# A router chain in a new order of statements, and a new end that keeps the last sums in PSUM

## The chip, the cores and the metric

The kernel runs on one core of a Trainium2 chip. The metric is the device time of one execution in microseconds (us); of three runs the median counts. A profiled execution has a span, from its first to its last recorded instruction, and a time of its own that is a little longer.

## What is computed

Two transformer blocks on 256 tokens of width 1024, in float32. The change touches the end of the second block: its mixture of 32 experts, of which a router picks four for each token, and the last normalisation.

```python
def moe_ffn(h, w_router, b_router, w1, b1, w2, b2):
    ...
    logits = (hf @ w_router + b_router).astype(jnp.float32)
    top_v, top_e = lax.top_k(logits, TOP_K)
    gates = jax.nn.softmax(top_v, axis=-1)
    ...
    def expert_block(args):
        xi, e = args
        hc = xi @ w1[e] + b1[e]
        g, u = hc[:, :D_EXPERT], hc[:, D_EXPERT:]
        g = jnp.minimum(g, SWIGLU_LIMIT)
        u = jnp.clip(u, -SWIGLU_LIMIT, SWIGLU_LIMIT)
        hm = (u + 1.0) * (g * jax.nn.sigmoid(SWIGLU_ALPHA * g))
        return hm @ w2[e] + b2[e]
...
        x = x + g1 * (mixed @ w_out[l])

        h2 = rms_norm_2(x, norm2_g[l]) * (1.0 + sc2) + sh2
        x = x + g2 * moe_ffn(h2, w_router[l], b_router[l], w_exp_in[l], b_exp_in[l], w_exp_out[l], b_exp_out[l])
    return rms_norm_2(x, final_g)
```

## The kernel before

The kernel goes through both blocks stage by stage; each stage's weights come through SyncE's DMA queue in the order of use, into a ring of seven slots of 2 MB and, for halves of the second expert weights, slots of 1 MB. A load is issued (L1116) when the instruction that last read its slot has ended. Engines run their own instructions in program order; TensorE (PE) does all products, VectorE (DVE) and ScalarE (ACT) read PSUM and do the elementwise work, GpSimd (POOL) does the powers that give reciprocal roots.

**Setup of the router.** The router's weights `wr` are multiplied once by the modulation's scale, and its constant row `crow` comes from the shift and the bias (`router_setup`, L1217). It runs as background work between other statements of block 2.

**Router.** The last product of the attention half leaves X in four PSUM banks, tile tt of 128 tokens by half of the width. `router_bank` (L1462) takes each bank as it ends: add it to X, transpose four blocks of 128 into PSUM, copy them to `xT` (which lies in `sg`), square X for the mean, and multiply with `wr` into 32 logits a token, one product for each of the eight blocks of the width. `choose` (L1451) scales the logits, finds the largest eight, their indices, and marks the four chosen in `sel`. `positions` (L1775) counts, by products with a triangle and with ones, which slot of its expert a token has; `one_hots` (L1532) makes the 64 slots' one-hot columns P, and `dispatch` (L1542) gathers the tokens for a pair of experts by products of X and P into `px`, which ACT copies with the modulation to `xe`. A row `g2` is spread over the partitions by two 512-column products between the router's logits and the positions (L167, `pc` and `ph`, with ACT copies into `rowg`).

**Experts.** The loop at L1840 goes through p = 0 to 31, two experts to a pair. Stage 1 is 16 products, `pg` and `pu` in turn for the eight blocks kt, each as two half-width tiles of the array side by side, and a bias. Stage 2 (L1640) transposes the gated rows (`ph`), copies them to `hT` and multiplies them with the second weights into `py`, whose rows 0 to 63 hold the left 512 columns and rows 64 to 127 the right ones. `scaled2` (L1683) weights `py` with `rowg` into `ys`, the even expert in rows 0 to 63, the odd one in rows 64 to 127. `combine` (L1710) adds a pair into Y by four 512-column products with the transposed gate table `pt` (`weights_T` of `Pg`), each followed by an addition on DVE. It runs a pair late, in the next even expert; for the last pair it runs at the end.

**End.** `final` (L1910) follows each of those last four additions: Y times the gain `fg`, a square with its sum, and after the fourth the mean, the power and the scale. A loop for tokens that found no slot (L1930) runs as often as a value says, and then two DMAs write the output, one from SyncE's queue and one from ACT's (L1955).

In the order's rows and the profile one helper, L167, records every float32 product; names tell them apart. A 512-column product of 128 rows shows as two records in the timeline.

## Time and profile before

| | us |
|---|---|
| median of three runs | 2325.98 (2325.09 to 2327.9) |
| profiled execution, its own time | 2323.74 |
| its span | 2321.7 |
| PE busy in the span | 2216.9 |
| DVE busy | 1261.6 |
| ACT busy | 857.4 |
| share of 16 DMA engines, SyncE's queue | 70.5% |
| router, last product of block 2's attention half to first expert product | 1364.8 to 1380.0 |
| experts 0 to 31 | 1380.0 to 2307.2 |
| end, last product to the end of the span | 2307.2 to 2321.7 |

In a timeline a row has a start, a duration, the engine, the line, the operation, what it writes and reads with its shape, how many records were put together, and in brackets how long the engine was idle ahead of it and what it waited for. PE stands for products, PEld for loading their stationary operand. A stretch's row gives busy times and, as PEclk, the granted clock as a share of 2.4 GHz.

### The profile page before, as it was taken

How to read it: one execution, taken by the hardware profiler on the slowest of the kernel's cores; microseconds unless marked ns; L12 is line 12 of the kernel's file. 1: busy time of each engine (PE TensorE's matmuls, PEld its weight loads, DVE VectorE, ACT ScalarE, POOL GpSimd, SP SyncE). 2: the span in 40 equal slices, each digit the busy share in tenths (PEclk: the TensorE clock that was granted, in tenths of full speed). 3: DMA queues.
4: the chain of work that ended last, by engine and by line, in shares of the span. 5: the costliest groups of instructions: out<-in, count | busy, mean ns of one | idle time of the engine just before them, and what ended most of it. 6: DMA issues, size and time to landing. Idle time of an engine off the chain costs nothing.

```text
span 2321.7 us, 33945 instructions
## 1 busy us (share of the span) xinstructions
PE 2216.9 (95%) x13354; PEld 1571.5 (68%) x13354; DVE 1261.6 (54%) x2338; ACT 857.4 (37%) x1535; POOL 286.4 (12%) x316
## 2 busy tenths in 40 slices
PE   8999999999999999999999999999988888999997
PEld 7889999999999988888788863333333333433332
DVE  6677668897777677876687553422222222222223
ACT  5567454545777654544554531011000000000001
POOL 3003000202777400000032010000000000000000
PEclk9999999999999999999999999999999999999999
DMA  6434555555333578886455469999999999999996
GB/s 219 160 109 146 179 186 180 182 182 182 129 130 141 199 279 285 289 285 232 166 189 200 146 235 424 407 429 429 428 429 429 428 429 429 428 419 414 429 429 260
DMA packets 71376, 654.31 MB, mean 282 GB/s; under 512 B 8176, under 2 KB 8304, under 8 KB 15920
## 3 DMA queue, kind: packets, MB, share of 16 engines
q1 hardware_dynamic: 69264, 644.91, 70.5%
q0 software_dynamic: 1664, 6.56, 0.8%
q8 instruction: 106, 1.74, 0.3%
q10 hardware_dynamic: 288, 0.67, 0.1%
q14 instruction: 54, 0.44, 0.0%
HBM read 649.61 MB, written 2.49 MB: 281 GB/s over the span
## 4 chain that ended last, share of the span: by engine, by line
PE 57%; DMA 10%; DVE 4%; ACT 3%; issue 1%; POOL 0%; ACTq 0%; POOLq 0%; DVEq 0%; SPq 0%
PE acc L153 15%; PE lin L153 11%; DMA w<-in_w_exp_in 10%; PE py L167 8%; PE pg L167 7%; PE pu L167 7%; PE psR L167 2%; PE pc L167 2%; PE px L167 2%; PE psS L167 1%; DVE lo L122 1%; ACT hT L1647 1%; DVE cv L1262 1%; ACT xe L1553 1%; DVE Pg L1561 0%
## 5 line engine op out<-in xcount | busy, mean ns | idle before, releaser
L122 DVE TENSOR_TENSOR lo<-raw,hi 128x1024 fp32r<-128x1024 f32 x411 | 519.3, 1264 | 205.2 <-PE acc L153 92.0
L119 ACT ACTIVATE hi<-raw 128x1024 fp32r<-128x1024 f32 x411 | 434.4, 1059 | 300.8 <-PE acc L153 171.9
L153 PE MATMUL lin<-hbH,hi 128*128 128x256 f32 x1152 | 329.5, 286 | 0.0
L153 PE MATMUL lin<-hbL,hi 128*128 128x256 f32 x1152 | 325.5, 283 | 0.1
L153 PE MATMUL lin<-hbH,lo 128*128 128x256 f32 x1152 | 325.4, 282 | 0.0
L1601 ACT ACTIVATE sgm<-g 128x512 f32<-128x512 f32 (+1 forms) x34 | 20.8, 612 | 726.9 <-DVE g L1600 726.9
L167 PE MATMUL pg<-w,xe 128*64 128x512 f32 x1024 | 265.0, 596 | 22.1 <-DMA w<-in_w_exp_in 22.1
L167 PE MATMUL pu<-w,xe 128*64 128x512 f32 x1024 | 263.2, 592 | 0.0
L1600 DVE TENSOR_SCALAR g<-pg 128x512 f32<-128x512 f32 (+1 forms) x33 | 22.3, 675 | 403.9 <-PE pg L167 403.9
L153 PEld LDWEIGHTS lin<-hbH,hi 128*128 128x128 f32 x1152 | 218.9, 190 | 0.2 <-ACT hbH L764 0.2
L153 PEld LDWEIGHTS lin<-hbL,hi 128*128 128x128 f32 x1152 | 216.0, 188 | 0.3 <-DVE hbL L765 0.3
L153 PEld LDWEIGHTS lin<-hbH,lo 128*128 128x128 f32 x1152 | 216.2, 188 | 0.0
L153 PE MATMUL acc<-hi,wh 128*128 128x512 f32 x512 | 200.8, 392 | 0.0
L153 PE MATMUL acc<-hi,wl 128*128 128x512 f32 x512 | 199.5, 390 | 0.7 <-DVE wl L964 0.7
L153 PE MATMUL acc<-lo,wh 128*128 128x512 f32 x512 | 199.2, 389 | 0.0
L167 PEld LDWEIGHTS pg<-w,xe 128*64 128x64 f32 x1024 | 70.4, 137 | 173.3 <-issue 127.8
L1687 DVE TENSOR_TENSOR ys<-py,rowg 64x512 f32<-64x512 f32 x62 | 42.7, 688 | 242.1 <-PE py L167 241.6
L167 PEld LDWEIGHTS pu<-w,xe 128*64 128x64 f32 x1024 | 73.7, 137 | 146.0 <-issue 138.6
L153 PE MATMUL lin<-hH,hi 128*128 128x256 f32 x552 | 167.9, 304 | 0.0
L153 PE MATMUL lin<-hH,lo 128*128 128x256 f32 x552 | 159.8, 290 | 4.0 <-DVE lo L122 4.0
L153 PE MATMUL lin<-hL,hi 128*128 128x256 f32 x552 | 159.3, 289 | 1.0 <-DVE hL L1178 1.0
L167 PE MATMUL py<-w,hT 128*64 128x512 f32 x496 | 115.6, 609 | 21.6 <-ACT hT L1647 21.6
(549 smaller groups left out, 3614.4 us busy)
## 6 DMA issues: line engine op xcount, KB each, us to landing
w<-in_w_exp_in SPq DMA_DIRECT2D x128, 2048.0 KB, 25.8
raw<-in_peer_uT SPq DMA_DIRECT2D x64, 1024.0 KB, 4.8
raw<-in_peer_v SPq DMA_DIRECT2D x64, 1024.0 KB, 6.2
raw<-in_w_exp_out SPq DMA_DIRECT2D x64, 1024.0 KB, 22.6
w<-in_w_exp_out SPq DMA_DIRECT2D x32, 2048.0 KB, 29.3
raw<-in_w_in SPq DMA_DIRECT2D x48, 1024.0 KB, 4.8
whole<-in_w_ada SPq DMA_DIRECT2D x48, 512.0 KB, 6.4
raw<-in_w_out SPq DMA_DIRECT2D x8, 1024.0 KB, 4.9
```

Of the source, the lines that this page charges most:

```text
L119: nc.scalar.activation(it["hi"], r, AF.Copy)
L122: nc.vector.tensor_tensor(out=it["lo"], in0=r, in1=it["hi"].bitcast(F32), op=OP.subtract)
L153: PE.matmul(ps, l, r, start=start and n == 0, stop=stop and n == len(trios) - 1, skip_group_check=True)
L167: PE.matmul(ps, lhsT, rhs, start=start, stop=stop, skip_group_check=True)
L1262: V.scalar_tensor_tensor(dst, x_, cw[:, b, k:k + 1], dst, op0=OP.mult, op1=OP.add)
L1553: ACT.activation(xe[:, kt].rearrange("p e c -> p (e c)"), px[:, k], AF.Identity, scale=mc[:, 2, kt:kt + 1], bias=mc[:, 3, kt:kt + 1])
L1600: V.tensor_scalar(c(g), c(pg), 7.0, None, op0=OP.min)
L1601: ACT.activation(c(sgm), c(g), AF.Sigmoid, scale=1.702)
L1647: ACT.activation(hT[:, b], ph[:, b], AF.Copy)
L1687: V.tensor_tensor(out=ys[par * C:(par + 1) * C, c], in0=py[r], in1=rowg[r, c], op=OP.mult)
```

## The change

- `router_setup` moves to block 1's PEER stage, behind the modulation's columns (L1047); it is otherwise the same.
- The router is written as one sequence of statements by hand. The transposed X lies in `aH` and `aL`. The logits come by `product`: four products at a time with a quarter of the array's columns each (32 experts by 128 tokens), then a copy and one product with four stacked identity blocks (`ones4`) that adds the quarters and transposes. `choose` marks the four by replacing the four largest values and comparing; indices are found later. One square moves from ACT to DVE. The one-hots of the first pair are made in the router, and half of the first `px` and the row g2 move into stage 1 of expert 0.
- The last expert leaves the loop. Both transposed tables, the pair's `pt` and one for the last expert alone (`pt2`, the same 64 columns in both halves of its rows), are made ahead of its stage 1. In that stage the four sums of the output are begun in four PSUM banks: Y by a product with the identity, and expert 30's rows by one with `pt`. Behind its last product one DVE operation weights all of `py` in its own layout, and four half-height products add it to the sums. Squares, gains and scales read the sums, and four ACT copies then write them to Y for the loop of extra tokens.
- Both output DMAs go through SyncE's queue.

```diff
+        def router_setup():
+
+            e = XA[:, 0].rearrange("p (k e) -> p k e", k=8)
+            er = XA[:, 1, :32]
+            GP.tensor_tensor(out=e, in0=wr, in1=mc[:, 3, :, None].to_broadcast([128, 8, 32]), op=OP.mult)
+            yield 3
+            GP.tensor_tensor(out=wr, in0=wr, in1=mc[:, 2, :, None].to_broadcast([128, 8, 32]), op=OP.mult)
+            V.tensor_reduce(out=er, in_=e.rearrange("p k e -> p e k"), axis=AX.X, op=OP.add)
+            yield 3
+            pr = psM.tile([128, 512], F32, name="psM")
+            mm(pr[:, :32], ones, er, True, False)
+            yield 1
+            mm(pr[:, :32], col("b_router_2")[:32].to_broadcast([32, 128]), ident[:32, :32], False, True)
+            yield 1
+            ACT.activation(crow, pr[:, :32], AF.Copy)
...
+        xT = [keep.tile([128, 4, S], F32, name=n) for n in ("aH", "aL")]
+        tb = [psT.tile([128, 512], F32, name="psT"), psO.tile([128, 512], F32, name="psO")]
...
+        def product(i):
+
+            tt, half = divmod(i, 2)
+            if half == 0:
+                pl[tt] = lin.tile([128, 512], F32, name="lin")
+            for k in range(4):
+                r = slice(32 * k, 32 * k + 32)
+                mm(pl[tt][r, :128], wr[:, 4 * half + k], xT[half][:, k, tt * 128:tt * 128 + 128], half == 0, half == 1)
...
+        def logits(tt):
+
+            lT = scratch("ry")[:, :128]
+            ACT.activation(lT, pl[tt][:, :128], AF.Copy)
+            mm(pl[tt][:, 128:128 + NR], lT, ones4, True, True)
...
+            V.tensor_copy(out=v4[:, tt, :4], in_=v8[:, tt, :4])
+            V.match_replace(out=eq[:, tt, 0], in_to_replace=v4[:, tt], in_values=lg[:, tt], imm_value=-3.0e38)
+            V.tensor_scalar(sel[:, tt], eq[:, tt, 0], -2.0e38, None, op0=OP.is_lt)
...
+        ended = [bank0, bank1, bank2, lambda: iter(())]
+        wide_tokens(ps, (mH, mL), 8, lambda i: bg.add(ended[i]()))
         bg.drain()
+        mean(0)
+        moved(3)
+        turn(1)
+        copy(1)
+        square(2)
+        square(3)
+        product(0)
+        turn(2)
+        product(1)
+        copy(2)
+        turn(3)
+        logits(0)
+        copy(3)
+        mean(1)
+        choose(0)
+        product(2)
+        product(3)
+        logits(1)
+        choose(1)
+        positions(0)
+        positions(1)
...
-                if kt == 0:
-                    dispatch(pair, 0, 2)
+                if kt < 2:
+                    dispatch(pair, 0, 2, kt)
...
+                    for _ in row([(psc, "pc"), (psc, "pc")], "g2", rowg):
+                        pass
...
+    p = NE - 1
+    hs = lambda dh: slice(dh * 512, dh * 512 + 512)
+    pt = weights_T(Pg)
+    cl = columns(p // 2, posm, perm[:, 0:2]), columns(p // 2, gate, perm[:, 2:4])
+
+    pt2 = weights_T(weights(*[lambda tt, e, f=f: f(tt, 1) for f in cl]))
+    last = work.tile([128, 8, 2, C], F32, name="xe").rearrange("p (a k) e c -> p a (k e c)", a=2)
+    rowg2, ysl = last[:, 0], last[:, 1]
+    for dh in range(2):
+        r = slice(64 * dh, 64 * dh + 64)
+        GP.tensor_copy(out=rowg2[r], in_=rowg[r, hs(dh)])
+    sums = [(psc if i < 2 else psx).tile([128, 512], F32, name="pc" if i < 2 else "px") for i in range(4)]
+
+    def before(kt):
+        if kt in (3, 5):
+            tt = kt // 4
+            for dh in range(2):
+                mm(sums[2 * tt + dh], ident, Y[:, tt, hs(dh)], True, False)
+                mm(sums[2 * tt + dh], pt[:C, tt], ys[:C, hs(dh)], False, False)
+
+    u = stage1(lambda kt: pair[1][:, kt, 1], ohp[:, order[p]:order[p] + 1], fetch, before, cuts=2)
+    stage2(u, fetch, None, 1, cuts=2, scaled=lambda py: V.tensor_tensor(out=ysl, in0=py, in1=rowg2, op=OP.mult))
     O = stream.rawp.tile([128, 2 * D], F32, name="raw").rearrange("p (a c) -> p a c", a=2)
     fss = wr[:, :2, :4]
+    for tt in range(2):
+        for dh in range(2):
+            r = slice(64 * dh, 64 * dh + 64)
+            mm(sums[2 * tt + dh], pt2[r, tt], ysl[r], False, True)
...
+    for f, i in ((squares, (0, 0)), (gains, (0, 0)), (squares, (0, 1)), (gains, (0, 1)), (squares, (1, 0)), (gains, (1, 0)),
+                 (squares, (1, 1)), (rstd, (0,)), (gains, (1, 1)), (scale, (0,)), (rstd, (1,)), (scale, (1,))):
+        f(*i)
+    for i in range(4):
+        ACT.activation(Y[:, i // 2, hs(i % 2)], sums[i], AF.Copy)
...
-        (nc.sync, nc.scalar)[t].dma_start(out=out[t * 128:(t + 1) * 128], in_=O[:, t])
+        nc.sync.dma_start(out=out[t * 128:(t + 1) * 128], in_=O[:, t])
```

PE between the second bank's transposes and the first expert matmuls, before. `sg` holds the transposed X, `modr` with `ident` spreads the row g2, `scr` is the triangle:

```order
L167 MATMUL lin<-wr,sg 128x32 x8
L1471 MATMUL psO<-ident,X 128x128 x4
L167 MATMUL lin<-wr,sg 128x32 x8
L167 MATMUL pc<-modr,ident 128x512
L167 MATMUL ph<-modr,ident 128x512
L167 MATMUL pc<-sel,scr 128x32
L167 MATMUL pc<-sel,ones 128x32
L167 MATMUL pc<-sel,scr 128x32
L167 MATMUL px<-P,X 128x128 x8
L167 MATMUL pg<-w,xe 64x512 x2
L167 MATMUL pu<-w,xe 64x512 x2
```

PE from the last bank's transposes on, after; `aH`, `aL` hold the transposed X, `qk` the partial logits, and `wr` now holds the one-hots where `px` reads it:

```order
L1516 MATMUL psO<-ident,X 128x128 x4
L167 MATMUL lin<-ones_12125,qk 128x32
L167 MATMUL lin<-aH,wr 32x128 x4
L167 MATMUL lin<-aL,wr 32x128 x4
L167 MATMUL lin<-ones_12125,qk 128x32
L167 MATMUL lin<-sel,scr 128x32
L167 MATMUL lin<-sel,ones 128x32
L167 MATMUL lin<-sel,scr 128x32
L167 MATMUL px<-wr,X 128x128 x4
L167 MATMUL pg<-w,xe 64x512 x2
L167 MATMUL pu<-w,xe 64x512 x2
L167 MATMUL px<-wr,X 128x128 x4
```

The logits are quarter-array products of 128 columns in the place of eight products of 32, the transposes of the third and fourth bank stand between them, the row g2 is gone from here and the first expert matmuls stand behind a quarter of `px`.

PE at the start of expert 31, before, from the late sums of the pair before on:

```order
L167 MATMUL pc<-ys,pt 128x512 x4
L1644 MATMUL ph<-ident,g 128x128 x4
L167 MATMUL py<-w,hT 64x512 x8
L167 MATMUL py<-raw,hT 64x512 x8
L167 MATMUL pg<-w,xe 64x512 x2
L167 MATMUL pu<-w,xe 64x512 x2
L167 MATMUL pg<-w,xe 64x512 x2
```

The same place after:

```order
L167 MATMUL py<-w,hT 64x512 x8
L167 MATMUL py<-raw,hT 64x512 x8
L1638 MATMUL px<-ident,Pg 128x128 x4
L167 MATMUL pg<-w,xe 64x512 x2
L167 MATMUL pu<-w,xe 64x512 x2
L167 MATMUL pg<-w,xe 64x512 x2
L167 MATMUL pu<-w,xe 64x512 x2
L167 MATMUL pg<-w,xe 64x512 x2
L167 MATMUL pu<-w,xe 64x512 x2
L167 MATMUL pc<-Y,ident 128x512
L167 MATMUL pc<-ys,pt 128x512
L167 MATMUL pc<-Y,ident 128x512
```

Four transposes of gate tables stand ahead of the stage, and identity and `pt` products inside it; a second such group of four follows after the fifth pair of `pg` and `pu`.

DVE from the weighting of expert 30 on, before:

```order
L1687 TENSOR_TENSOR ys<-py,rowg 64x512 x2
L1600 TENSOR_SCALAR g<-pg 128x128x2
L1602 TENSOR_SCALAR pu<-pu 128x128x2
L1603 SCALAR_TENSOR_TENSOR g<-pu,g 128x128x2
L1604 TENSOR_TENSOR g<-g,sgm 128x128x2
L1600 TENSOR_SCALAR g<-pg 128x128x2
L1602 TENSOR_SCALAR pu<-pu 128x128x2
L1603 SCALAR_TENSOR_TENSOR g<-pu,g 128x128x2
L1604 TENSOR_TENSOR g<-g,sgm 128x128x2
L1571 COPY pt<-px 128x256
```

The same place after:

```order
L1757 TENSOR_TENSOR ys<-py,rowg 64x512 x2
L1639 COPY pt<-px 128x256
L1629 TENSOR_SCALAR Pg<-iota,perm 128x64 x4
L1639 COPY pt<-px 128x256
L1668 TENSOR_SCALAR g<-pg 128x128x2
```

The copy of `pt` has moved ahead of the gated rows of expert 31, and four operations for a second table with one more copy stand behind it.

## Rows read from the trace of the kernel before

**Rows 1.** Stretches, all engines: busy us, granted TensorE clock (PEclk), DMA share, GB/s.

```profile
core 0: us, PE busy (x) PEld busy (x) DVE busy (x) ACT busy (x) POOL busy (x), PEclk, DMA share, GB/s
1373.00:1379.60 6.60, 6.54 (x24) 5.08 (x23) 3.96 (x18) 2.00 (x4) 1.25 (x3) 0.50 0.99 336
1640.00:2004.00 364.00, 326.07 (x1570) 128.94 (x1566) 81.28 (x159) 34.94 (x77) 0.00 (x0) 1.00 1.01 429
2004.00:2280.00 276.00, 262.19 (x1357) 101.44 (x1358) 64.97 (x131) 24.27 (x53) 0.00 (x0) 0.98 1.00 424
2270.70:2274.10 3.40, 3.40 (x8) 1.48 (x6) 1.38 (x2) 0.00 (x0) 0.00 (x0) 0.50 1.00 429
2282.00:2295.50 13.50, 13.50 (x64) 4.43 (x62) 1.38 (x2) 0.00 (x0) 0.00 (x0) 1.00 1.00 423
```

**Rows 2.** Timeline of the router, all engines: start us, duration us, engine, line.

```profile
1366.16 0.69 DVE L1468 TENSOR_TENSOR X<-qk,X 128x512 f32<-128x512 f32 x1
...
1367.86 0.59 ACT L1478 ACTIVATE sg<-psT 128x512 f32<-128x512 f32 x1
...
1368.74 0.70 PE L1471 MATMUL psO<-ident,X 128*128 128x128 f32 x4
...
1372.04 1.14 PE L167 MATMUL pc<-modr,ident 128*128 128x512 f32 x2
...
1373.15 0.25 DVE L1453 SCALAR_TENSOR_TENSOR lg<-lin,rs,crow 128x32 f32<-128x32 f32 x1 [0.68 <-POOL rs L228]
...
1374.50 0.37 DVE L1459 TENSOR_REDUCE sel<-eq 128x32 f32<-128x128 f32 x1
...
1376.01 4.07 PE L167 MATMUL px<-P,X 128*128 128x128 f32 x16
...
1378.56 0.81 ACT L1553 ACTIVATE xe<-px,mc 128x128 f32<-128x128 f32 x2 [3.03 <-PE px L167]
...
1380.01 1.08 PE L167 MATMUL pg<-w,xe 128*64 128x512 f32 x4
...
1396.56 2.15 PE L167 MATMUL px<-P,X 128*128 128x128 f32 x16
```

**Rows 3.** What SyncE's DMA queue waited for, 1360 to 1395 us.

```profile
SPq L1116 <- PE lin L167: 7.0, 1, 7.0
```

**Rows 4.** Timeline around the start of the last expert (p = 31).

```profile
2265.77 1.98 PE L167 MATMUL pc<-ys,pt 128*128 128x512 f32 x4
...
2268.45 0.97 DVE L1561 TENSOR_SCALAR Pg<-iota,perm 128x64 f32<-128x64 f32 x4
...
2270.07 3.22 PE L167 MATMUL pc<-ys,pt 128*128 128x512 f32 x4 [2.32 <-DVE Y L1720]
...
2281.81 1.03 PE L167 MATMUL pg<-w,xe 128*64 128x512 f32 x4
...
2282.03 1.39 DVE L1687 TENSOR_TENSOR ys<-py,rowg 64x512 f32<-64x512 f32 x2 [8.01 <-PE py L167]
...
2296.08 0.44 PE L1570 MATMUL px<-ident,Pg 128*128 128x128 f32 x2
...
2299.47 0.42 DVE L1571 COPY pt<-px 128x256 f32<-128x256 f32 x1
```

**Rows 5.** Timeline of the end, after the last product of expert 31.

```profile
2307.98 3.90 PE L167 MATMUL pc<-ys,pt 128*128 128x512 f32 x8 [0.79 <-DVE ys L1687]
...
2313.18 0.63 ACT L1915 ACTIVATE g<-Y 128x512 f32<-128x512 f32 x1
...
2314.59 0.72 POOL L228 TENSOR_TENSOR wr<-wr,nhalf 128x2 f32<-128x2 f32 x1 [0.90 <-DVE wr L1919]
...
2318.02 0.36 ACTq L1955 DMA_DIRECT2D out_dram<-raw  x1
```

**Rows 6.** The router's setup before: its group on VectorE, and 1200 to 1220 us.

```profile
L1223 DVE TENSOR_REDUCE lg<-eq 128x32 f32<-128x256 f32 x1 | 0.6, 585 | 0.0
...
1200.00:1220.00 20.00, 17.77 (x121) 16.44 (x120) 19.16 (x29) 12.27 (x22) 9.75 (x10) 0.94 0.52 200
```

More of the change, by code (lines that the diff above doesn't have):

```diff
@@ new lines, in choose, with positions @@
+            V.tensor_scalar(sel[:, tt], eq[:, tt, 0], -2.0e38, None, op0=OP.is_lt)
+        def positions(tt):
+            pp = lin.tile([128, 512], F32, name="lin")
+            if tt:
+                mm(pp[:, :NR], ones, sel[:, 0], True, False)
+            mm(pp[:, :NR], utri, sel[:, tt], tt == 0, True)
+            V.scalar_tensor_tensor(posm[:, tt], pp[:, :NR], 1.0, sel[:, tt], op0=OP.add, op1=OP.mult)
+            for e in range(2):
+                e0 = order[0] + e
+                V.tensor_scalar(P0[:, tt, e], iota[:, 1:C + 1], posm[:, tt, e0:e0 + 1], rs[tt], op0=OP.is_equal, op1=OP.mult)
@@ L1472, in router_bank @@
-            xk = xT[:, 4 * half:4 * half + 4, t]
-            tk = tb[i].rearrange("p (k t) -> p k t", k=4)
-            if i == 3:
-                V.tensor_copy(out=xk[:, :2], in_=tk[:, :2])
-                ACT.activation(xk[:, 2:], tk[:, 2:], AF.Copy)
-            else:
-                ACT.activation(xk, tk, AF.Copy)
-            ACT.activation(scratch("rj"), x, AF.Square, accum_out=ss[tt][:, half:half + 1])
-            if half:
-                mean(tt)
-            if not pl:
-                pl.append(lin.tile([128, 512], F32, name="lin"))
@@ L1484, in router_bank, with square @@
-            if i:
-                yield (None, 1.3, 1.0, 1.0)[i]
-                logits(tt, range(4 * half if tt else 0, 4 * half + 4))
-            if half:
-                yield 0
-                choose(tt)
-        GP.tensor_scalar(utri, diff, 0.0, None, op0=OP.is_gt)
-        wide_tokens(ps, (mH, mL), 8, lambda i: bg.add(router_bank(i)))
-        bg.drain()
+            V.tensor_tensor(out=X[:, tt, c], in0=y, in1=X[:, tt, c], op=OP.add)
+        def square(i):
+            tt, half = divmod(i, 2)
+            x = X[:, tt, half * 512:half * 512 + 512]
+            if i == 3:
+                V.scalar_tensor_tensor(scratch("rj"), x, 1.0, x, op0=OP.mult, op1=OP.mult, accum_out=ss[tt][:, half:half + 1])
+            else:
+                ACT.activation(scratch("rj"), x, AF.Square, accum_out=ss[tt][:, half:half + 1])
@@ new lines, in turn, with copy, bank0 @@
+        def turn(i):
+            tt, half = divmod(i, 2)
+            for k in range(4):
+                PE.transpose(tb[i % 2][:, k * 128:(k + 1) * 128], X[:, tt, kslice(4 * half + k)], ident)
+        def copy(i):
+            tt, half = divmod(i, 2)
+            x = xT[half][:, :, tt * 128:tt * 128 + 128]
+            t = tb[i % 2].rearrange("p (k t) -> p k t", k=4)
+            ACT.activation(x, t, AF.Copy)
+        def bank0():
+            moved(0)
+            square(0)
+            yield 0.7
+            turn(0)
+            copy(0)
@@ L1540, in one_hots, with dispatch @@
         return P, work.tile([128, 8, 2, C], F32, name="xe")
-    def dispatch(pair, half, parts=1):
+    def dispatch(pair, half, parts=1, only=None):
         P, xe = pair
         n = 4 // parts
-        for i in range(parts):
+        for i in range(parts) if only is None else [only]:
             px = psx.tile([128, n, 2 * C], F32, name="px")
@@ L1773, in tile_kernel @@
     GP.dma_start(out=b2t, in_=a["b_exp_out_2"])
[L1774 to L1786 removed]
+    pair = P0, work.tile([128, 8, 2, C], F32, name="xe")
+    def gate_values():
+        for tt in range(2):
+            V.max_index(out=i8[:, tt], in_max=v8[:, tt], in_values=lg[:, tt])
+        V.tensor_copy(out=iF, in_=i8)
+        for tt in range(2):
+            V.tensor_tensor(out=eq[:, tt], in0=iF[:, tt, :4, None].to_broadcast([128, 4, NE]),
+                            in1=iota[:, None, :NE].to_broadcast([128, 4, NE]), op=OP.is_equal)
         g4 = small.tile([128, 2, 4], F32, name="g4")
@@ L1907, in tile_kernel, with junk, squares, gains @@
     O = stream.rawp.tile([128, 2 * D], F32, name="raw").rearrange("p (a c) -> p a c", a=2)
     fss = wr[:, :2, :4]
+    for tt in range(2):
+        for dh in range(2):
+            r = slice(64 * dh, 64 * dh + 64)
+            mm(sums[2 * tt + dh], pt2[r, tt], ysl[r], False, True)
+    def junk():
+        return work.tile([128, 512], F32, name="g", bufs=1)
+    def squares(tt, dh):
+        ACT.activation(junk(), sums[2 * tt + dh], AF.Square, accum_out=fss[:, tt, dh:dh + 1])
+    def gains(tt, dh):
+        V.tensor_tensor(out=O[:, tt, hs(dh)], in0=sums[2 * tt + dh], in1=fg[:, hs(dh)], op=OP.mult)
```

100 lines of the change are left out of this document (43 added, 57 removed).

## Prediction

> **What bounds the kernel now.** I read the stretches first: for each the busy time of every engine, the granted clock and the DMA share. From 1640 to 2004 us TensorE (PE) is busy for 326 of 364 us while the DMA share is 1.01 at 429 GB/s: the weight stream leads and PE waits for it. From 2004 to 2280 us PE is busy for 262 of 276 us, and through stage 1 of the last expert, 2282.0 to 2295.5, for 13.50 of 13.50 us at full clock [rows 1]. No wait of PE for a DMA is left there, so whatever PE is given in expert 31 has no cover. Second, the timeline of the router: it is a serial chain over PE, ScalarE (ACT) and VectorE (DVE) [rows 2]. Third, the timeline around the start of the last expert and that of the end, both serial too [rows 4, 5]. So three places count: the chain ahead of expert 0, stage 1 of expert 31, and what follows its last product.
>
> **Router chain.** Before, X is complete at 1366.85 (1366.16 + 0.69), the last four transposes start only at 1368.74, the second tile's logits are scaled at 1373.15, its choice ends at 1374.87 and the first expert matmul starts at 1380.01 [rows 2]. After, rs of tile 0 and the DVE square stand near the last X; I let X end at about 1367.2 and the transposes of bank 3 start 0.4 later. Then: transposes 0.70, ACT copy 0.59 (the rows' durations), four 32-row products that can share the array about 0.4, the ACT copy of their partial logits about 0.4 and the product with the stacked ones about 0.2 (a copy of a quarter of the columns; a 32-column product like those that took 1.08 for eight): 1369.9. The choice keeps its first step of 0.25 and has three shorter ones instead of index, cast, compare and reduce: about 1.0 in place of 1.72 (1373.15 to 1374.87). It ends near 1371.1, 3.8 us earlier. From a choice's end to the first px product took 1.14, to which I add 0.4 for the second tile's two one-hots: 1372.65. The first px took 4.07 for 16 records at half clock and takes 2.15 at full clock [rows 2]; now only a quarter of the 32 stands ahead of the first expert matmul: 1.05 (full) to 2.0 (half). With one ACT copy, half of the 0.81 for two, the first pg starts at about 1375.0, 5.0 us earlier.
>
> Not all of that is kept. Stage 1 of expert 0 now also holds the other half of the first px (1.05) and the two 512-column products of row g2, which lay beside the choice at 1372.04: by the price of such products in p30, 1.98 for two or 0.86 as the step of the pg row, 1.7 to 2.0. And one more copy-to-matmul handover of about 0.45. Kept: 5.0 − 1.05 − 1.7 − 0.45 = **1.8 us**. Bounds: granted clock 0.50 over 6.6 us, 1373.0 to 1379.6, followed 32-column products and gaps on PE [rows 1]. If it does not fall now, 3.3 us of half-speed work comes back and the gain is up to 5.1; if it falls again and reaches into expert 0's 512-column matmuls, the gain is 0. I take 1.8, since the new chain has gaps of the same kind.
>
> **The queues it passes.** The first weight load of expert 1 no longer waits for the logits' reading of sg: SyncE's queue waited 7.0 us for that [rows 3]. It starts about 7 us earlier and the stream's early idle closes. But the ring has a fixed number of slots, and the stream is released by PE later in the first experts; so I let the DMA-led stretch up to 2004, and the PE-led one behind it, move by PE's 1.8 only.
>
> **Setup moved.** It takes a DVE reduce of 0.585, two POOL products, two small matmuls and a copy out of a stretch where DVE is busy for 19.16 of 20 us [rows 6], and puts them behind the modulation columns, where PE's long products lead. Gain 0 to 0.6 there, cost 0 to 0.6 here: **0 ± 0.6**.
>
> **Stage 1 of expert 31.** Two things are added ahead of or into it, on PE in order.
> (a) The transposes of both weight tables stand ahead of the first pg. The second table (only the last expert's rows) is built by four DVE operations, queued behind the two ys of expert 30 and the first table's copy. Its price: py of expert 30 ends where pg starts now, 2281.8; ys start at 2282.03 and take 1.39, the copy 0.42, the four Pg 0.97 and two transposes 0.44 [rows 4]. With handovers that is 2285.3 in place of 2281.81: **+3.5 us**, of which PE idles about 2.6. ACT and DVE have nothing else that waits then, but all of stage 1 is queued behind the transposes.
> (b) Eight 512-column products: four of the identity on Y and four of pt on expert 30's rows. Before, expert 30's rows were combined together with expert 31's in four products behind the last py; these four stay as half-height ones, so all eight are extra. At 0.86 to 0.98 each [rows 4]: **+6.9 to 7.8**; I take 6.9, since they stand between pg matmuls at that step.
> (c) The clock. A wait of 2.32 us of PE at 2267.75 was followed by granted clock 0.50 over 3.4 us, which cost 1.7 [rows 1, 4]. The new wait is 2.6 us long. Bounds 0 to 1.7; **+0.8**.
>
> *A rule against this.* Behind px (128 wide) the trace shows pg (64 wide) at the matmuls' own step: 4.07 from 1376.01 ends at 1380.08 and pg stands at 1380.01 [rows 2]; a change of width costs nothing visible, and my sum has nothing for it. The Trainium skill, TensorEngine Tiling (Array Packing), Key Properties, says that changing the tiling mode drains TensorE; the router's quarter-array products among whole-array transposes, and the wide products in expert 31's stage 1, would change it some dozen more times. What that would give is the third rival.
>
> **The end.** Before: the last py ends at 2307.2 (T), the sums take 3.90 from 2307.98, the fourth square starts at 2313.18, the power takes 0.72 from 2314.59, the second output DMA starts at 2318.02 and the span ends at 2321.7: T + 14.5 [rows 5]. After: one weighting of 0.69, the half-height sums in two pairs done by T + 1.9 and T + 3.0 if two share the array, four squares at a step of 0.75 to 0.8 from T + 2.1, so done by T + 5.3; then the last gain 0.69, scale 0.45, mean 0.3, power 0.6 to 0.72, scale 0.66 on ACT: T + 8.1. Then ACT copies the four sums into Y, and the output DMAs behind the loop of the extra experts wait for them: 4 at 0.5 to 0.63 (a square's time), T + 10.1 to 10.6. Both DMAs go through SyncE 0.35 apart; from the last issue to the end is 3.7: T + 14.2 to 14.7. Gain **0.2**, bounds −0.7 to +2.3 (all four copies hidden).
>
> **Sum.** −1.8 (router) + 0 (setup) + 3.5 + 6.9 + 0.8 (expert 31) − 0.2 (end) = +9.2 us. On the profiled run's 2323.74 that is 2332.9; the median of the runs shown is 2.24 above that run, so 2325.98 + 9.2 = **2335.2**.
>
> **Rivals.**
> 1. *Faster: the weight stream, not PE, sets expert 31.* For it: the DMA share is 1.00 from 2004 to 2280. Then the added 11.2 us fall into waits for weights, and the stream moves up by what the first slot's release gains, 5.1 at most. 2325.98 − 5.1 − 0.2 = 2320.7. It decides once expert 31's first weights land later than 2285.3 less the advance. Against: PE 13.50 of 13.50 busy in that stage [rows 1], and no DMA wait of PE since 2004. Chance 0.12.
> 2. *No change that can be told: the whole advance of the router is kept* and the clock holds in both places. PE does the router at full clock (−5.1), row g2 and the second px finding gaps (−2.0), the wait of (a) leaves 2.6: 2325.98 − 5.1 − 2.0 + 2.6 + 6.9 − 0.2 = 2328.2. For it: PE has gaps in the first expert. Against: DVE's order in front of the second table is fixed. Chance 0.18.
> 3. *Slower by more: a change of array width costs.* As a mechanism here: PE would finish all that is in flight before a product of another width. Between px and pg the rows show 0 for it; its other end is one short operation, 0.44 as for the two transposes at 2296.08 [rows 4]. With some eight changes that no other wait covers: 8 × 0.4 = +3.2, so 2338.4. Chance 0.07. It is the rule named above.
> 4. *The reordering does not shorten the router*, as the half clock reaches into expert 0: the gain of 1.8 goes, 2337. Inside my forecast's range; chance 0.1, counted with it.
>
> **How the numbers follow.** Forecast with rival 4: 0.61 (2331 to 2339); rival 3: 0.07; within: 0.18; faster: 0.12; 0.02 for something above 2341. A measurement of this kernel tells about 0.2%, 4.65 us, from no change: slower 0.70, same 0.18, faster 0.12. The range leaves out the faster case and what is above 2340: 2325 to 2340.
>
> **What would show it.** Right: in the trace after, a PE wait of 2 to 3 us for DVE between the last py of expert 30 and its pg; eight more products of 512 columns in stage 1 of expert 31, which then lasts 20 to 21 us instead of 13.7; first pg about 5 us after the choice of the second tile ends near 1371; ACT's four copies ahead of the output DMAs. Wrong: PE waiting for weights in expert 31, stage 1 of expert 31 no longer than 14 us, or a first pg that moved up by much more than 5 us and kept it to 2004.

## The result, and the profile after

The changed kernel takes 2341.78 us (median of four, 2339.37 to 2344.57) against 2325.53 us: ratio 1.0068, 95% interval 1.0053 to 1.0083. It is slower, as forecast, but by 16 us and not by 9, and 1.8 us above the end of the range. The profiled execution has a span of 2337.4 us, 15.7 more than before. I followed the lead of the trace after over the trace before (how much earlier it reaches the same instruction, the nth of a kind on its engine). In the table, half clock is a granted clock of 0.50, 1.2 GHz in place of 2.4, and landing is the moment at which a transfer's data has arrived. The lead splits the 15.7 us:

| stretch | before | after | difference |
|---|---|---|---|
| 1095 us to the last product of the attention half | 269.5 | 265.5 | −4.0 |
| from there to the gated rows of expert 0 | 31.6 | 30.0 | −1.6 |
| experts 1 to 21, where PE waits for weights | | | +3.3 |
| expert 22, half clock 10.2 us in place of 6.8 | | | +1.6 |
| experts 23 to 30 | | | −0.2 |
| last py of expert 30 to the first pg of expert 31 | −0.2 | 3.3 | +3.5 |
| stage 1 of expert 31 | 14.0 | 24.1 | +10.2 |
| from there to the first py | 4.3 | 4.5 | +0.2 |
| py of expert 31 | 7.1 | 9.5 | +2.4 |
| from there to the landing of the output | 13.65 | 14.1 | +0.5 |

These sum to 15.9; 0.2 us of lead that the trace after has at 1095 us already stands against it. The timeline of the kernel after around the start of expert 31 answers to [rows 4]; start, duration, engine, line, and in brackets the wait:

```profile
2280.78 0.44 PE L1638 MATMUL px<-ident,Pg 128*128 128x128 f32 x2
2280.89 1.39 DVE L1757 TENSOR_TENSOR ys<-py,rowg 64x512 f32<-64x512 f32 x2 [8.00 <-PE py L167]
2282.30 0.42 DVE L1639 COPY pt<-px 128x256 f32<-128x256 f32 x1
2282.74 0.98 DVE L1629 TENSOR_SCALAR Pg<-iota,perm 128x64 f32<-128x64 f32 x4
2283.33 0.92 PE L1638 MATMUL px<-ident,Pg 128*128 128x128 f32 x2 [2.11 <-DVE Pg L1629]
2284.18 1.98 PE L167 MATMUL pg<-w,xe 128*64 128x512 f32 x4
...
2289.91 1.03 PE L167 MATMUL pu<-w,xe 128*64 128x512 f32 x4
2290.86 1.13 PE L167 MATMUL pc<-Y,ident 128*128 128x512 f32 x2
2291.92 1.12 PE L167 MATMUL pc<-ys,pt 64*128 64x512 f32 x2
2292.97 1.12 PE L167 MATMUL pc<-Y,ident 128*128 128x512 f32 x2
2294.03 1.12 PE L167 MATMUL pc<-ys,pt 64*128 64x512 f32 x2
2295.08 1.08 PE L167 MATMUL pg<-w,xe 128*64 128x512 f32 x4
...
2310.43 0.51 PE L1712 MATMUL ph<-ident,g 128*128 128x128 f32 x2 [1.74 <-DVE g L1672]
...
2312.23 0.67 PE L1712 MATMUL ph<-ident,g 128*128 128x128 f32 x2 [1.30 <-DVE g L1672]
2312.83 6.07 PE L167 MATMUL py<-w,hT 128*64 128x512 f32 x16
```

The chain ys, copy, four Pg, transposes stands there as the sum had it, and pg starts 3.3 us behind py. The eight added products step by 1.055 us (2290.86, 2291.92, 2292.97), not by 0.86; at each of them the part of the array that is used changes, 128*128 for Y and 64*128 for ys, of which below. The first pg (1.98 us) and the first half of py (6.07) are slow. In the trace before the first half of py took 3.65:

```profile
2300.11 3.65 PE L167 MATMUL py<-w,hT 128*64 128x512 f32 x16
```

The stretches of the kernel after say why (columns as in [rows 1]):

```profile
1369.50:1373.90 4.40, 4.34 (x18) 1.81 (x18) 0.46 (x3) 0.35 (x2) 0.00 (x0) 0.69 1.03 361
...
1640.00:1990.00 350.00, 310.98 (x1467) 118.67 (x1466) 75.70 (x148) 32.12 (x71) 0.00 (x0) 1.00 1.01 427
...
2283.60:2287.00 3.40, 3.28 (x10) 1.16 (x11) 0.54 (x2) 0.00 (x0) 0.00 (x0) 0.50 1.02 434
2287.00:2308.00 21.00, 21.00 (x75) 6.19 (x74) 0.00 (x0) 0.00 (x0) 0.00 (x0) 1.00 0.46 194
2310.90:2317.70 6.80, 5.50 (x15) 1.79 (x16) 0.99 (x3) 0.92 (x3) 0.00 (x0) 0.50 0.00 0
```

Half clock for 3.4 us behind the wait of 2.1 us, and for 6.8 us behind the two waits for the gated rows. And from 1640 us the stream runs at 427 GB/s; it was 429 [rows 1]. The router:

```profile
1363.95 0.43 PE L167 MATMUL lin<-aL,wr 128*32 128x128 f32 x8
...
1367.31 0.50 PE L167 MATMUL px<-wr,X 128*128 128x128 f32 x2 [0.21 <-DVE wr L1494]
...
1369.56 1.98 PE L167 MATMUL pg<-w,xe 128*64 128x512 f32 x4 [0.61 <-ACT xe L1621]
...
1372.74 1.21 PE L167 MATMUL px<-wr,X 128*128 128x128 f32 x8
...
1375.74 2.15 PE L167 MATMUL px<-wr,X 128*128 128x128 f32 x16
...
1381.41 1.98 PE L167 MATMUL pc<-modr,ident 128*128 128x512 f32 x4
```

The first pg stands 8.9 us behind the end of the last product of the attention half (1360.67), where it was 15.2 (1364.82 to 1380.01 [rows 2]); the rows below it are what came into stage 1 in return, px and the row g2.

### The profile page after: what moved, and what is told of

It is laid out like the page before. It is cut to its first block, busy times and chain, and to the rows that moved or that the text cites. A ratio compares the mean times of both kernels' runs of the same rounds, so it can differ in the third digit from the quotient of the medians.

```text
span 2337.4 us, 34008 instructions
## 1 busy us (share of the span) xinstructions
PE 2223.4 (95%) x13376; PEld 1566.5 (67%) x13376; DVE 1262.4 (54%) x2348; ACT 858.8 (37%) x1539; POOL 289.3 (12%) x322
## 4 chain that ended last, share of the span: by engine, by line
PE 56%; DMA 11%; DVE 4%; ACT 2%; issue 1%; POOL 0%; SPq 0%; ACTq 0%; POOLq 0%; DVEq 0%
PE acc L153 15%; DMA w<-in_w_exp_in 11%; PE lin L153 11%; PE py L167 7%; PE pg L167 7%; PE pu L167 7%; PE psR L167 2%; PE px L167 2%; PE pc L167 2%; PE psS L167 1%; DVE lo L122 1%; ACT hT L1715 1%; ACT xe L1621 1%; DVE Pg L1629 0%; DVE cv L1269 0%
```

## Which part costs what

**The whole change again**, for a second trace:

> The changed kernel as it is, once more. Against the kernel before it took 16 us more (2341.8 against 2325.5). Its trace was 5.8 us ahead at the end of stage 1 of expert 0, but only 0.9 us ahead from expert 22 on: the lead shrank by 3.3 us between 1644 and 2000 us, where PE waits for weights. Theory A, the stream of weights is slower by chance of an execution (427 against 429 GB/s): then this profile shows another lead at expert 22, by 1 us or more, with the same code. Theory B, the change makes it so: the lead at expert 22 is 0.9 us again, within 0.5. Both expect the time at 1.005 to 1.008 of the kernel before.

2343.07 us, 1.0075 (1.0056 to 1.0094). The lead shrank by 3.3 us between 1644 and 1997 us again, at 426 GB/s: B, the change makes the stream slower. It had 13.7 us of half clock ahead of the router where the first trace had 6.8, and 6.8 in the router for 3.4: these falls do differ between executions.

**The new router and the moved setup, with the old end** (the last expert back in the loop, `combine(*prev[:2], then=final)` behind it, two output queues):

> The new router and the moved setup, with the old end (last expert in the loop, its pair's sums behind the last product, two output queues). Theory A, the loss is all in expert 31 and the end: 0.94 us to 5.8 us faster than the kernel before, 2320 to 2324.6, ratio 0.9975 to 0.9996. Theory B, the early part costs something too (the stream, the clock at expert 22): 2325.5 or more. The lead at expert 0 should be 5.8 us by both, what is left of it at expert 31 tells.

2327.05 us, 1.0009 (0.9999 to 1.0018). So most of the slowdown is the end's; but none of the lead of 3.6 us at expert 0 is left. 2.6 went in the stream, and behind it 1.7 in half clock in py and 1.8 in the landing of the output, of which below.

**The new end alone**, on the kernel before:

> The new end alone, old router and setup. Theory A, the end costs what the traces differ by in it, whatever stands before: from expert 31's first product on 3.4 us of wait for DVE, 8.4 of eight added products at 1.055 each, 1.6 and 2.5 of half clock after waits, 0.5 in the last stretch, 16.6 in all: 2342, ratio 1.0072. Theory B, the two falls of the clock come from where the clock stood when the router's lead met them: 4 us less, 2338. My prediction's price for the end would be 10.9 us: 2336.5.

2339.62 us, 1.0054 (1.0037 to 1.0070). From py of expert 30 to the landing it takes 54.4 us, as in the second trace of the change, against 38.9 in the trace before: 15.5 more. The ratio gives 12.6, the number of theory B, but not its mechanism: the 6.8 us of half clock behind the gated rows are there again, only the fall behind the tables' wait is not. The trace before is an exception there: of the nine traces of the old end whose waits are as they were, it alone has no half clock in py of expert 31. The second trace of before (below) has 3.4 us of it and takes 40.6, which leaves 13.8 for the new end. The stream here runs at 429 GB/s.

**The setup's move alone:**

> The router's setup moved behind the modulation's columns, old router and old end. The trace of the changed kernel is 4.6 us ahead of the one before already at the last product of block 2's attention half, ahead of all router changes, and has 6.8 us of half clock there in place of 17.1 us. Theory A, the move does it (the crowded stretch of DVE at 1200 us is free): 4 to 5 us ahead at 1360 us, and what the stream leaves of it at the end, 0.5 to 4 us faster, 2321.5 to 2325. Theory B, falls of the clock are chance of an execution: less than 1.5 us ahead at 1360 us in this profile, 2325 to 2326. My prediction said 0 within 0.6.

2328.08 us, 1.0004 (0.9994 to 1.0014). Neither theory as it stood: 1.5 us ahead at 1360 us, and 2.9 behind from expert 22 on. The stream runs at 426 to 427 GB/s, so it is the setup's move, not the router, that slows the stream.

## The place of the ring's slots

The move takes `crow`, 128 bytes a partition, from one SBUF pool into another above it. Everything between lies 128 bytes lower, the four slots of the first weight ring too: at 156288 and on in place of 156416. The old addresses are multiples of 256, the new ones lie 128 above one. Between 1480 and 2000 us the time from one landing to the next shows it (us, medians of 12 or 13 loads of 2 MB into each slot; in brackets where the slots lie, counted from a multiple of 256):

| trace | the four slots of the first ring | the three others of 2 MB |
|---|---|---|
| before | 4.83 to 4.85 (+0) | 4.89 to 4.90 (+128) |
| after | 4.89 to 4.90 (+128) | 4.89 to 4.90 (+128) |
| after, with the line below | 4.84 to 4.86 (+0) | 4.89 to 4.90 (+128) |
| old end, all slots moved (further below) | 4.84 to 4.85 (+0) | 4.84 to 4.85 (+0) |

Only these two places were tried. One line of padding moves the four slots by another 128 bytes, to 156160 and on:

```diff
+        V.memset(modp.tile([128, 32], F32, name="padr"), 0.0)
```

> The new router and setup with the old end, as in the run before, and 128 bytes of padding on the right side of SBUF, so that the four slots of the first weight ring start at multiples of 256 bytes again, as in the kernel before. (The row crow had moved from one pool to another and had shifted them by 128.) Theory A, the place of the slot sets the stream: loads into these four slots take 4.84 us in place of 4.895, the stream runs at 429 GB/s in place of 427, and of the 3.6 us of lead at expert 0 some 3 are kept to expert 22: 2323 to 2325. Theory B, the slower stream has another cause in the moved setup: 4.895 us and 427 GB/s as in the run before, 2326 to 2328.

> The changed kernel with the same 128 bytes of padding. Theory A (place of the slots): the lead at expert 0 is kept to within 0.5 us up to 1997 us, loads into the four slots take 4.84 us, and the time falls by 2.5 to 3.5, to about 2338.5 to 2339.5. Theory B: nothing changes, 2341 to 2343.

2324.48 us, 0.9996 (0.9987 to 1.0005), for the old end and 2337.72 us, 1.0050 (1.0038 to 1.0062), for the changed kernel. Both traces keep their lead: 2.3 us at expert 0 and 2.7 at 1997 us, 4.5 and 4.4. The stretches of the changed kernel with the padding:

```profile
1640.00:1990.00 350.00, 313.02 (x1486) 120.73 (x1486) 76.81 (x150) 32.76 (x72) 0.00 (x0) 1.00 1.01 429
```

Theory A, then; some 3.3 us of the change's 16 were never in its instructions. The Trainium skill, DMA: Bandwidth & Descriptors, How a descriptor splits into AXI transactions, says that a transaction must start at a multiple of 256 bytes, so that the first transaction of a descriptor which starts elsewhere begins at the boundary below. It speaks of the reading side. By it a row of 16 KB as one descriptor would need 65 transactions in place of 64, 1.6%, as an estimate from that page. The loads here write SBUF and show 1.1%; why is not shown.

The left side's slots (three of 2 MB, three of 1 MB) were at odd multiples of 128 all along. Packing four small tiles into one and leaving out a fifth, a padding, moves them by 128 bytes:

```diff
+    tiny = const.tile([128, 8], F32, name="tiny")
+    eps5 = tiny[:, 0:1]
...
+    nhalf = tiny[:, 1:2]
...
-    V.memset(const.tile([128, 8], F32, name="pad"), 0.0)
...
+        r = tiny[:, 2 + int(name[2]):3 + int(name[2])] if pl is const else pl.tile([128, n], F32, name=name)
```

> As the old end with padding, and the constants packed into 128 bytes less, so that the left side's slots (three of 2 MB, three of 1 MB) start at multiples of 256 bytes too. Theory A: all loads of 2 MB take 4.84 us, the stream runs at about 431 GB/s, and the stretch from 1644 to 2000 us, where PE waits for it, is 2 to 3 us shorter than with the four slots alone: 2320.5 to 2323, ratio under 0.9985. Theory B: no difference to the run with the four slots.

> The kernel before with the left side's slots moved to multiples of 256 bytes by the packed constants, nothing else; its right side's four slots are there already. Theory A: loads into the left slots take 4.84 us in place of 4.895 and 2 to 3 us are gained between 1644 and 2000 us: 2323 to 2324.5, ratio about 0.999. Theory B: no difference.

2318.36 us, 0.9964 (0.9951 to 0.9977), and 2319.50 us, 0.9972 (0.9960 to 0.9983). All slots of 2 MB now take 4.84 to 4.87 us, the stream runs at 430 GB/s, and 1.8 to 1.9 us are gained between 1644 and 1997 us. That is less than the gain in time. The rest is in block 1: between 340 and 820 us, where PE is busy for 479 of 480 us, all seven traces with the left side moved gain 5.4 us, bit by bit, and none of the others gains any. All left tiles moved with the slots, also those that PE reads there; which of them matters was not tried.

## Expert 31

All four have the padding and are to be read against 1.0050. The first moves the tables to where DVE has had time for them (`begin` starts two of the four sums):

```diff
+        if kt == 1:
+            T[0] = weights_T(Pg)
+            T[2] = weights(*[lambda tt, e, f=f: f(tt, 1) for f in cl])
+        if kt == 3:
+            T[1] = weights_T(T[2])
+            begin(0)
```

> The changed kernel with padding, and expert 31's two table transposes moved into its stage 1, behind the first and behind the third pair of products, where DVE has had time for them. Theory A: PE's wait of 2.1 us and the start that was 3.4 us late go, and with them the fall of the clock over 3.4 us that followed (1.6 us): 4 to 5 us less than the padded kernel's 1.0050 of the kernel before, 1.0029 to 1.0033. Theory B, the clock falls in that place anyway (it did not in one of two traces, where the wait was the same): 3.0 to 3.4 us less, 1.0036.

2334.99 us, 1.0034 (1.0023 to 1.0046). In the trace pg follows py without a gap, 3.5 us earlier, as predicted, and no fall of the clock follows there:

```profile
2279.77 0.60 PE L167 MATMUL py<-raw,hT 128*64 128x512 f32 x2
2280.20 1.02 PE L167 MATMUL pg<-w,xe 128*64 128x512 f32 x4
...
2285.97 0.44 PE L1639 MATMUL px<-ident,Pg 128*128 128x128 f32 x2
2286.24 1.02 PE L167 MATMUL pc<-Y,ident 128*128 128x512 f32 x2
...
2287.20 1.12 PE L167 MATMUL pc<-ys,pt 64*128 64x512 f32 x2
```

Of the 3.5 us 0.6 come back: stage 1, with the transposes in it, lasts 23.4 us where it lasts 22.75 with them ahead of it (no fall of the clock in either).

The second also moves one group of four products behind stage 1:

```diff
+    begin(1)
     stage2(u, fetch, None, 1, cuts=2, scaled=lambda py: V.tensor_tensor(out=ysl, in0=py, in1=rowg2, op=OP.mult))
```

> As the run with the tables late, and the second group of four products (identity on Y and pt on expert 30's rows for the second half of the tokens) moved from stage 1 to just behind it, where PE waits 1.7 us and 1.3 us for the gated rows. Theory A, the waits there let the clock fall for 6.8 us in the last products (all three traces of the new end show it): filling the gap saves about 3.0 us of waiting and 3.4 of half clock, so 4 to 6 us less than the run with the tables late, 1.0005 to 1.0015. Theory B, the fall there has another cause: 2.5 to 3 us less.

2329.43 us, 1.0013 (1.0004 to 1.0022). Its timeline:

```profile
2303.47 1.12 PE L167 MATMUL px<-ys,pt 64*128 64x512 f32 x2
2304.52 0.51 PE L1713 MATMUL ph<-ident,g 128*128 128x128 f32 x2
...
2305.56 0.51 PE L1713 MATMUL ph<-ident,g 128*128 128x128 f32 x2 [0.53 <-ACT hT L1716]
2306.00 3.65 PE L167 MATMUL py<-w,hT 128*64 128x512 f32 x16
```

Both waits for the gated rows are gone and py runs at full clock, 7.1 us. Against the run before it, stage 1 is 4.4 us shorter and the way to py 1.7 longer. The half clock in py is not shown by this pair, since the trace of the tables late has none there either, though its two waits, 1.7 and 1.3 us, are as they were. The medians are 5.6 us apart, of which the traces explain 2.7.

The third leaves the eight products out (Y and expert 30's rows are missing from its output):

> The changed kernel with padding, with the eight products in stage 1 of expert 31 left out: Y and expert 30's rows are missing from the output. Theory A, each costs PE 1.055 us and has no cover: stage 1 ends 8.4 us earlier against the last product of expert 30, 1.0014 of the kernel before. Theory B, as the prediction priced them, 0.86 each: 6.9 us. Whether stage 1 then lasts 15.4 us (13.7 and one fall of the clock) tells A from B.

2329.89 us, 1.0012 (1.0003 to 1.0022). Stage 1 lasts 14.0 us without a fall of the clock; with the products and without a fall (second trace of the change, and the run below) it lasts 22.75. That is 8.7 us for eight, 1.09 each. They are not slower by themselves: where whole-array products follow one another, their records, two to a product, start 0.43 us apart, so a product steps by 0.86 as a pg does. Two sums and the two fillers of a run below show it, the second pair starting 1.83 us behind the first (0.1 of it at the start of the first) and taking 1.88, three steps of 0.43 and a last record of 0.59:

```profile
2258.01 1.98 PE L167 MATMUL pc<-ys,pt 128*128 128x512 f32 x4
2259.84 1.88 PE L167 MATMUL px<-X,ident 128*128 128x512 f32 x4
```

In stage 1 each group of four changes the used part of the array five times: 128*64 to 128*128, to 64*128, back, again, and to 128*64. At a change the step into it and the step behind it are longer, 0.52 and 0.53 us (0.47 where pg follows) in place of 0.43. Eight at 0.86 are 6.9, and the other 1.9 are ten changes at 0.19. In the trace of the tables late (above) the first sum stands behind transposes of its own form, and steps by 0.96 in place of 1.055. So my third rival was right in kind: the Trainium skill, TensorEngine Tiling (Array Packing), Key Properties, says that changing the tiling mode drains TensorE, and the trace agrees with a price of 0.19 us a change. No run has the eight products without the changes.

The fourth leaves out the four copies into Y, which only the loop for tokens without a slot would read:

> The changed kernel with padding, without the four ACT copies into Y at the end (the loop of extra tokens, which does not run on these inputs, would miss them). Theory A, the output DMAs wait for them: the first is issued 2.0 to 2.2 us earlier behind the last product and the time falls by as much, 1.0041. Theory B, the end waits for something else: less than 0.5 us, 1.0050.

2336.34 us, 1.0040 (1.0026 to 1.0053). The first output DMA starts 8.42 us behind py in place of 10.18.

## The first half again, and the waits filled

> The kernel before once more, for its trace. Theory A, without the setup's move TensorE's clock falls more often between 1095 us and the last product of the attention half: 17 us or more of half clock there again. Theory B, chance: as likely under 14 us as over. By both, that stretch takes 262.4 us and 0.45 for each us of half clock.

> The setup moved, with the old router and the old end, and all ring slots at multiples of 256 bytes. Against the run with the left slots in place and nothing else (ratio 0.9972) it differs by the setup's move alone. Theory A, fewer falls: half clock before the router at most 13.7 us and a ratio lower by 0.001 to 0.0015, 0.9957 to 0.9962. Theory B, the move is worth nothing: 0.9972 within 0.0008.

> The new router alone, setup where it was, old end, all ring slots at multiples of 256 bytes. Against the run with the left slots in place (0.9972) it differs by the router alone. Theory A, the early start is given back in stage 1 of expert 0: from the last attention product to the end of that stage 30.0 us with 3.4 of half clock or 31.5 with 6.8, 0.1 to 0.7 less than the old router, ratio 0.9969 to 0.9972. Theory B, the lead of 5.8 us at the first expert product is kept by the weight loads that start 7 us earlier: 0.9950.

2325.58 us (one run); 2319.93 us, 0.9969 (0.9959 to 0.9980); 2321.10 us, 0.9980 (0.9971 to 0.9989). Neither the setup's move nor the router can be told from the kernel before with its left slots in place (0.9972); but their outputs land 1.3 and 2.1 us later than its output does, for another reason (last section). From the last attention product to the gated rows of expert 0 the old router takes 31.65 us with 6.8 of half clock and 30.8 (30.7 to 31.3) with 3.4; the new one 31.5 and 30.0. **By its traces at equal half clock the router is worth 0.1 to 0.8 us.** Ahead of it the stretch from 1095 us takes about 262.4 us (261.7 to 262.9) and 0.45 for each us of half clock, with the setup moved or not. The half clock there is 10 to 24 us in the six traces without the move and 7 to 24 in the fourteen with it, 16.5 and 12 in the mean; the second trace of before has 17, but so has the moved setup with all slots in place. Whether the move makes falls rarer stays open.

Last, the waits of expert 31 filled with work that nobody reads, on the run with the old end and all slots in place:

```diff
+            if cuts == 2 and j % 2 == 0:
+                mm(psc.tile([128, 512], F32, name="pc"), ident, X[:, 0, :512], True, True)
             PE.transpose(ph[:, j], u[:, j:512:4], ident)
```

> As the old end with all slots in place (0.9964), and two products of 512 columns that nobody reads put into PE's waits for expert 31's gated rows, one ahead of the first two transposes and one ahead of the other two. Theory A, the idle time there is what lets the clock fall: no half clock in the last products of expert 31, which then take 7.1 us in place of 8.8, and the transposes start no later than before: 1.7 us less, 0.9957. Theory B, the fall has another cause: 8.8 us again, 0.9964 or a little more.

2314.27 us, 0.9944 (0.9930 to 0.9957), **12.7 us less than the kernel before and the lowest ratio of all**. The stretch around the waits and py, in the run without and with the filler:

```profile
2294.70:2303.00 8.30, 5.59 (x20) 2.15 (x20) 3.44 (x9) 1.55 (x4) 0.00 (x0) 0.80 0.04 15
```

```profile
2287.59 1.02 PE L167 MATMUL pc<-X,ident 128*128 128x512 f32 x2
2289.24 0.48 PE L1715 MATMUL ph<-ident,g 128*128 128x128 f32 x2 [0.62 <-DVE g L1673]
2289.55 1.02 PE L167 MATMUL pc<-X,ident 128*128 128x512 f32 x2
2290.96 0.48 PE L1715 MATMUL ph<-ident,g 128*128 128x128 f32 x2 [0.38 <-DVE g L1673]
2291.37 3.65 PE L167 MATMUL py<-w,hT 128*64 128x512 f32 x16
...
2291.00:2299.00 8.00, 7.46 (x34) 2.46 (x34) 0.65 (x2) 0.38 (x1) 0.00 (x0) 1.00 0.00 0
```

The transposes start no later, and py takes 7.1 us in place of 8.8. Of the 4.1 us between the medians of the two runs (4.7 by their ratios) the clock is 1.7; 1.5 is the landing of the output, which comes sooner here for another reason (below).

> As the run with the filler (0.9944), and two more products that nobody reads in PE's wait of 2.3 us for Y in expert 30's sums. Theory A, idle time lets the clock fall: no half clock between 2260 and 2300 us, 1.7 us less, 0.9937. Theory B, the fall there comes from something else (narrow work before it): half clock over 3.4 us again, 0.9944.

> The kernel before, its left slots at multiples of 256 bytes and the filler products in expert 31's waits; old router, setup and end. If the new router and the moved setup are worth what the traces show at equal half clock, 0.1 to 0.7 and 0, this comes out within 1.5 us of the run with both and the filler: 0.9944 to 0.9952. If they are worth what the changed kernel's lead of 5.8 us suggested: 0.9965 or more.

2316.32 us, 0.9954 (0.9940 to 0.9969), and 2319.89 us, 0.9969 (0.9958 to 0.9980). With the second filler the granted clock is 1.00 throughout:

```profile
2258.00:2300.00 42.00, 38.85 (x163) 13.99 (x162) 12.50 (x26) 2.79 (x6) 0.00 (x0) 1.00 0.73 310
```

All other traces have half clock there for 3.4 us or more, and the narrow work ahead of the wait is the same, so theory A is shown: the wait lets the clock fall. The time does not show it: 0.9954 and 0.9944 have overlapping intervals, and this trace has 3.4 us more of half clock in the router and again at expert 22.

The kernel before with slots and filler came out at 0.9969, where my expectation has the other theory, that router and setup are worth more than their traces show. Its trace, 3.4 us slower than that of the run with both and the filler, has 3.4 us more of half clock at expert 22 and again behind expert 30's sums (1.7 us each), and an output that lands 1.2 us later; 3.4 us of half clock fewer ahead of the router (1.5 us) stand against it. So the question stays open. Three pairs differ by router and setup together: the old end with padding against the kernel before, the same with the left slots moved, and this last pair. The ratios put the two 0.9, 1.9 and 5.8 us ahead, and with equal landings, if each trace's landing is that of its kernel, it would be 2.7, 3.4 and 4.6. Each has 2 to 4 us of interval on either side. Some 2 us of it could be the rarer falls ahead of the router (4.5 us of half clock in the mean, at 0.45), if the move makes them.

## Why the prediction was right in sign and wrong in size

- **Bound, and no cover in expert 31: right.** PE waited for no weights from 2004 us on after the change either, and what was added there showed in full.
- **The wait for the second table, +3.5: right**, 3.5 (3.4 in the second trace), and 3.5 came back when the tables were moved, less 0.6 in stage 1.
- **Eight products, +6.9: the price of a product was right, the changes put at nothing: a step that failed.** I had the step of 0.86, and that is what a whole-array product takes too. What I put at nothing were the changes of the used part of the array, ten of them, 1.9 us; measured 8.7 for all. I read "costs nothing visible" from px ending at 1380.08 and pg starting at 1380.01 [rows 2]. But records of one form overlap by 0.16 us (0.59 long, 0.43 apart), so an overlap of 0.07 was itself a loss. My third rival, at 0.07, had eight changes at 0.4; there were ten at 0.19.
- **The clock, +0.8: mis-sized, 3.9 in the first trace.** I saw the wait that the change adds (1.5 in that trace; no fall in the second, and in two of the six traces of the new end with its tables early). I had no term for the waits that stay. Behind the waits for expert 31's gated rows the trace before has no fall, but eight of the nine traces of the old end have one of 3.4 us, the second trace of before among them, and five of those six of the new end have 6.8. So 1.7 of the 3.9 is the luck of the one trace that I worked from.
- **Router, −1.8: small, for other reasons.** The first pg came 6.3 us earlier relative to the last attention product (I said 5.0), and 0.1 to 0.8 were kept at equal half clock by the traces, where I had 1.8. What came back into stage 1 was right in kind, but more: g2 took 2.0, and the half clock, which the old order spent on the narrow work ahead of the experts, now lay on the first expert products (0.69 from 1369.5 to 1373.9). The weight load was issued at 1361.13, 11.2 us earlier, without a wait for the logits, and brought nothing, as said.
- **Setup, 0: the step that failed most.** I put it at nothing from its instructions alone, which no run contradicts, and never priced the 128 bytes that it moves: they cost 3.3 us in the stream. The diff showed `crow` in another pool; I read that as nothing. With the slots in place the changed kernel takes 2337.72 us, 1.0050, which lies inside my range. In the first trace fewer falls of the clock ahead of the router hid it, which was luck: the second trace, 16 us slower as well, gains 1.3 there and not 4.0.
- **The end, −0.2: wrong by 0.7.** The copies are waited for, as I had it (1.8 us). The second output DMA, now behind the first on one queue, lands 3.5 us after its start in place of 2.8.

In the first pair of traces, against 9.2: 1.9 more for the changes of form, 3.1 for the clock, 0.7 for the end, and 0.9 for all that lies ahead of expert 31, where the stream's 3.3 and expert 22's 1.6 were nearly paid for by the 4.0 of fewer falls ahead of the router. That last and part of the clock are chance of two executions. As an estimate for the medians, 13.8 for the new end and 3.3 for the stream, less 0.1 to 0.8 for the router, make 16.3 to 17.0, where 16.2 was measured.

## What to carry to other kernels

An early start is worth what is still early at the next place that everything passes; read there, not at the first product that moved. Products added to the stage that bounds the kernel cost their full step, and each change of the used part of the array some more (0.19 us here); put them, or tables' transposes, where PE waits anyway. In the four kernels with the waits of expert 31 filled the clock did not fall there. When a tile changes its pool, look at what else changes its address.

## What the hardware showed that I had not expected

- **Slots at multiples of 256 bytes** take loads of 2 MB in 4.83 to 4.87 us, those 128 bytes above one in 4.89 to 4.90; where the stream leads, four of seven slots are worth 3.3 us in 350, for a line of padding.
- **Whole-array float32 products of 512 columns step by 0.86 us, as a pair of half-width ones does;** a change between forms costs 0.19.
- **Loading of code can lie in the last transfer.** In some kernels the first output DMA lands 3.8 to 4.8 us after its start, in others after 2.6 to 2.7, the same in kind and size. The DMA queues of the last 6 us, the kernel before and then the run with the old end:

```profile
q1 hardware_dynamic: 144, 0.52, 21.9%
q10 hardware_dynamic: 144, 0.52, 21.6%
issues: line engine op xcount, KB each, median us to landing
out_dram<-raw SPq DMA_DIRECT2D x1, 512.0 KB, 2.7
```

```profile
q8 instruction: 1, 0.02, 1.6%
issues: line engine op xcount, KB each, median us to landing
out_dram<-raw SPq DMA_DIRECT2D x1, 512.0 KB, 4.5
```

  In all eight traces with the slow landing a packet of code (q8) starts between the start and the landing of the output; in none of the twelve with the fast one does one start there (in three one had begun up to 0.9 us ahead). The Trainium skill, Runtime: NRT & Kernel Launch, Instruction fetch mechanics, says that an engine's instructions are refilled by DMA in blocks of 16 KiB; the packet's 0.02 MB agrees. So 1.2 to 2.1 us seem to go by where a block of a kernel's code ends. It was not tried by itself. The eight are the old end with its slots in each of the three places, the two runs of the setup's move, the router alone, the run without the eight products, and the kernel before with slots and filler; their times hold it.
- **Falls of TensorE's clock** differ between executions of one kernel, each worth 1.7 us or a multiple; single traces of this kernel can't be compared below some 4 us without counting them.
